# An expert block whose first stage is done by gathered rows, with its weights summed in DRAM

## The chip, the core and the metric

The kernel runs on one core of a Trainium2 chip. TensorE (PE) multiplies matrices, VectorE (DVE) and ScalarE (ACT) work on tiles of 128 partitions, GpSimd (POOL) works more slowly and issues the indirect transfers, and SyncE (SP) issues most of the plain ones. Each engine runs its instructions in a fixed order. The metric is the device time of the whole kernel in microseconds; lower is better.

## What is computed

One block of a language model works on 1,024 tokens of width 1,024 (eight blocks of 128 tokens). First come four mLSTM heads and four gMLP groups with an output projection; then a product-key layer (PEER) that picks, for each token and each of eight heads, 16 of 16,384 experts. The change touches only the second:

```python
s1, i1 = lax.top_k(s[:, :, 0], 16); s2, i2 = lax.top_k(s[:, :, 1], 16)
top_s, pos = lax.top_k(s1[..., :, None] + s2[..., None, :], 16)   # 16 of 16*16
idx  = i1 * 128 + i2 (at pos)                  # expert of the token: 8 heads x 16
gate = softmax(top_s)
a    = gelu(einsum('td,thkd->thk', x, expert_u[idx]))
out  = einsum('thk,thkd->td', a * gate, expert_v[idx])
```

## The kernel before

**Two ways through the experts.** A block can take the *sparse* way: for each of its 128 (head, choice) pairs, GpSimd gathers 128 rows of `u` (one for each token, 4 KB each) and VectorE takes the dot product with the normalised token (`dot`, L691 to L697); the same again with rows of `v`, weighted and added up (`add`, L707 to L713). Or it can take the *dense* way: every expert is computed for every token by TensorE, and a table of gates, zero for the experts that were not picked, is multiplied in. Blocks 0 to 4 are dense and blocks 5 to 7 sparse (`DENSE`, `SPARSE`).

**The front** (`front_part`, L563) works through parts of 2, 3 and 3 blocks: heads and groups, output projection, then the queries and scores of the experts. Weights come in half by half through three buffers (`wraw`, `split_w`, L66), each matrix is split into a high and a low part, and a product takes three matmuls (`mm3`, L89). The choice of experts of a block (`topk_units`, L452) and, for a dense block, its gate table (`gate_units`, L642) are side work: lists of small steps that `interleave` deals out between the main steps of the next part, the whole list within the first 210 cost units of that part. A gate step (a *quad*, four tokens) makes two tables of ones with VectorE (`AB`, L656), scales one with ScalarE (L659) and multiplies them on TensorE (`pG`, L661); 32 quads make a block's table, written to `d_G` in DRAM. The last list of side work is the choice of experts of block 5, which the main path runs itself.

**The dense stage** (`experts`, L755) has 128 expert rows of 128 experts, in 32 groups of four. `stage1` loads a row of `uT` (L777), splits it into `uhi` (ScalarE, L778) and `ulo` (GpSimd, L779), multiplies it with the 640 dense tokens in two halves of 320 columns (`pa`), and makes weights `wh`, `wl` of it with the gates `Gin`, which are loaded once a group (L771). `stage2` loads and splits four rows of `v` and adds their product to the accumulators of five blocks (`pout`, 2 x 512 columns for each block). The sparse blocks are side work of this stage: their gathers, dots and adds are dealt out between the expert rows, through seven row buffers (`gat`).

**What sets the order.** The code is emitted in the order of these loops, and a scheduler places the instructions of every engine by its own timeline of the program; `keep_in_program_order` pins the gathers among each other, and `high_priority` lifts a few steps. What the chip then does is in order, engine by engine.

Of the kernel before, what the change touches and what calls it, by code (L numbers as in the profile page):

```python
# [7 lines left out]
F32 = mybir.dt.float32  # L8
F32R = mybir.dt.float32r
# [7 lines left out]
DRAM = bass.MemoryType.DRAM  # L17

D = 1024
# [6 lines left out]
TG = 32  # L26

DENSE = [0, 1, 2, 3, 4]
SPARSE = [5, 6, 7]
# [11 lines left out]
NGAT = 4  # L41
# [5 lines left out]
class Build:  # L47
# [124 lines left out]
    def consts(self, cp):  # L172
# [9 lines left out]
        self.rall = cp.tile([128, 8], F32, name="rall", tag="rall")  # L182
        self.mhalf = cp.tile([128, 16], F32, name="mhalf", tag="mhalf")
# [269 lines left out]
    def topk_units(self, blk):  # L453
# [15 lines left out]
        def merge(h0):  # L469
            ijg = st["ijg"]  # L470
            self.merge16(h0, st["tv"], st["ti"], ijg)
            if blk in self.sparse:
                if h0 == 0:
                    self.pick[blk] = (self.kp.tile([128, 128], I32, name="ix", tag=f"ix{blk % 2}"),
                                      self.kp.tile([128, 128], F32, name="gt", tag=f"gt{blk % 2}"))
                ix, gt = self.pick[blk]
                hl = slice(h0 * 16, (h0 + HB) * 16)
                v.scalar_tensor_tensor(ix[:, hl], ijg[:, 0, hl], float(NEXP), ijg[:, 1, hl], op0=OP.mult, op1=OP.add)
                v.tensor_copy(gt[:, hl], ijg[:, 2, hl])

        def done():
            ijg = st["ijg"]
            if blk in self.dense:
# [74 lines left out]
    def front_part(self, part):  # L558
# [61 lines left out]
        for b in range(self.nb):  # L620
            blk = b0 + b
            if blk in self.dense:
# [19 lines left out]
    def gate_units(self, blk):  # L642
        nc = self.nc
        pool = self.gp
        s = self.dense.index(blk)
# [29 lines left out]

    def sparse_units(self, blk, pool, psum):
# [4 lines left out]
        def begin():  # L681
            st["ix"], st["gt"] = self.pick[blk]
# [55 lines left out]
    def open_x(self):  # L738
# [4 lines left out]
        T = len(self.dense) * 128  # L743
        self.xh = self.xp.tile([128, 8, T], F32R, name="xh", tag="xh")
        self.xl = self.xp.tile([128, 8, T], F32R, name="xl", tag="xl")
        for s, blk in enumerate(self.dense):
# [9 lines left out]
    def experts(self, side, dp, ps):  # L756
# [5 lines left out]
        T = ND * 128  # L762
        T2 = T // 2
        n32 = T // TG
        ngroups = NEXP // GS
        W, V, st = {}, {}, {"n": 0}

        def stage1(g, e):
            if e == 0:
                st["G"] = dp.tile([128, n32, GS, TG], F32, name="Gin", tag="Gin", bufs=1)  # L770
                nc.sync.dma_start(st["G"], self.d_G[:, :, g * GS:(g + 1) * GS].rearrange("n j i t -> j n i t"))  # L771
            G = st["G"]
# [9 lines left out]
            for s in range(2):  # L782
                pa = ps.tile([128, T2], F32, name="pa", tag="pa", bufs=3)
                sl = slice(s * T2, (s + 1) * T2)
                self.mm3(pa, [((uh[:, c], ul[:, c]), (xh[:, c, sl], xl[:, c, sl])) for c in range(8)])
                with self.first():
                    nc.scalar.activation(pa, pa, AF.Gelu_apprx_tanh)  # L787
                    p3 = pa.rearrange("p (n t) -> p n t", t=TG)
                    v.tensor_tensor(p3, p3, G[:, s * (n32 // 2):(s + 1) * (n32 // 2), e], op=OP.mult)  # L789
                    nc.scalar.activation(wh[:, sl], pa, AF.Copy)  # L790
                    v.tensor_sub(wl[:, sl], pa, wh[:, sl].bitcast(F32))  # L791
# [207 lines left out]
```

## Time and profile before

| | us |
|---|---|
| median of three runs | 2869.16 (2865.69 to 2877.17) |
| profiled execution | 2870.66 |
| its span | 2868.9 |
| busy in it: TensorE | 2707.1 (94%) |
| VectorE | 2198.3 (77%) |
| GpSimd | 1498.8 (52%) |
| ScalarE | 1120.5 (39%) |

The span is that of the profiled execution on the chip; the time around it is 1.8 us. Busy shares are means over stages with different limits, so they are read stage by stage below. Matmuls overlap, so that the duration of one is longer than its share of the time: their price is the step from one start to the next. "Idle before" names what ended an engine's wait.

### The profile page before, as it was taken

The page shows a single profiled execution, that of the slowest core. Times are in us where ns is not written, and L with a number is a line of the kernel's source. Part 1 is how long each engine was busy: PE and PEld are TensorE (multiplying, and loading weights), DVE is VectorE, ACT ScalarE, POOL GpSimd, SP SyncE. Part 2 cuts the span into 40 slices and gives each one's busy share as a digit, 9 for nine tenths or more (in the row PEclk, how much of TensorE's full clock was granted, in tenths as well). Part 3 has the DMA queues.
Part 4 walks back from the last instruction along what each step waited for, and adds up shares of the span by engine and source line. Part 5 has one row for each costly group of instructions (what it writes and reads, how often), then busy time and mean ns, then how long its engine had stood idle before and what let it go on. Part 6 is the DMA issues. An engine that isn't in the chain of part 4 may idle for free.

```text
span 2868.9 us, 44783 instructions
## 1 busy us (share of the span) xinstructions
PE 2707.1 (94%) x16283; PEld 2468.9 (86%) x16283; DVE 2198.3 (77%) x4981; ACT 1120.5 (39%) x2295; POOL 1498.8 (52%) x1220
## 2 busy tenths in 40 slices
PE   7888989999898799999999999999999999999998
PEld 7887989889898798889888888888888898889987
DVE  6649975289985677888797787978987777777774
ACT  5444788348888322223222222222222222222222
POOL 4430020000200186767767677667767777777873
PEclk9989999999999899999999999999999999999999
DMA  7797557866578798988989999898989999999992
GB/s 252 253 315 281 187 216 278 277 223 226 186 274 312 257 328 299 335 313 311 326 282 331 338 322 330 300 344 302 316 284 342 343 330 332 331 322 326 336 320 111
DMA packets 327821, 838.41 MB, mean 292 GB/s; under 512 B 25520, under 2 KB 161072, under 8 KB 315824
## 3 DMA queue, kind: packets, MB, share of 16 engines
q0 software_dynamic: 114048, 427.87, 40.4%
q1 hardware_dynamic: 190544, 347.91, 37.0%
q10 hardware_dynamic: 23008, 59.77, 5.3%
q8 instruction: 128, 2.10, 0.3%
q14 instruction: 93, 0.76, 0.1%
HBM read 746.32 MB, written 89.13 MB: 291 GB/s over the span
## 4 chain that ended last, share of the span: by engine, by line
PE 58%; DVE 19%; DMA 9%; ACT 5%; issue 5%; POOL 3%; SPq 1%; ACTq 1%; another core or an unknown queue 0%; POOLq 0%; DVEq 0%
PE pa L96 8%; PE pa L94 7%; PE pa L95 7%; PE pout L94 7%; PE pout L95 7%; PE pout L96 7%; DMA Gin<-d_G 4%; DVE gat L697 2%; PE pG L661 2%; DVE sacc L713 2%; DVE AB L656 2%; PE pq L94 2%; PE pq L96 2%; PE pq L95 2%; DMA wraw<-win 1%
## 5 line engine op out<-in xcount | busy, mean ns | idle before, releaser
L94 PE MATMUL pa<-xh,uhi 128*128 128x320 f32 x2048 | 639.3, 312 | 28.9 <-ACT uhi L778 14.9
L95 PE MATMUL pa<-xl,uhi 128*128 128x320 f32 x2048 | 637.1, 311 | 0.0
L96 PE MATMUL pa<-xh,ulo 128*128 128x320 f32 x2048 | 625.5, 311 | 5.4 <-POOL ulo L779 5.4
L94 PE MATMUL pout<-vhi,wh 128*128 128x512 f32 x1280 | 505.4, 400 | 23.0 <-DVE acc L816 11.1
L713 DVE SCALAR_TENSOR_TENSOR sacc<-gat,aw,sacc 128x1024 f32<-128x1024 f32 x384 | 492.3, 1282 | 27.4 <-DMA gat<-v,ix 22.3
L95 PE MATMUL pout<-vlo,wh 128*128 128x512 f32 x1280 | 509.0, 399 | 0.0
L96 PE MATMUL pout<-vhi,wl 128*128 128x512 f32 x1280 | 490.2, 398 | 0.0
L709 POOL DMA_INDIRECT gat<-v,ix x384 | 363.5, 947 | 239.8 <-DVE sacc L713 131.0
L697 DVE SCALAR_TENSOR_TENSOR gat<-gat,xn 128x1024 f32<-128x1024 f32 x384 | 459.5, 1213 | 20.0 <-DMA gat<-u,ix 19.8
L693 POOL DMA_INDIRECT gat<-u,ix x384 | 363.3, 946 | 209.5 <-DVE gat L697 104.3
L94 PEld LDWEIGHTS pa<-xh,uhi 128*128 128x128 f32 x2048 | 389.2, 190 | 43.2 <-DVE wl L791 16.1
L96 PEld LDWEIGHTS pa<-xh,ulo 128*128 128x128 f32 x2048 | 385.7, 190 | 12.9 <-POOL ulo L779 8.2
L95 PEld LDWEIGHTS pa<-xl,uhi 128*128 128x128 f32 x2048 | 389.3, 190 | 7.3
L779 POOL TENSOR_TENSOR ulo<-raw,uhi 128x1024 fp32r<-128x1024 f32 x128 | 308.7, 2413 | 145.6 <-ACT uhi L778 142.9
L801 ACT ACTIVATE vhi<-raw 128x1024 fp32r<-128x1024 f32 x128 | 131.7, 1052 | 487.5 <-PE pout L95 414.8
L802 POOL TENSOR_TENSOR vlo<-raw,vhi 128x1024 fp32r<-128x1024 f32 x128 | 307.9, 2416 | 22.7 <-ACT vhi L801 20.3
L94 PEld LDWEIGHTS pout<-vhi,wh 128*128 128x128 f32 x1280 | 242.0, 190 | 78.8 <-DVE acc L816 14.4
L816 DVE TENSOR_TENSOR acc<-acc,pout 128x512 f32<-128x512 f32 x320 | 214.2, 682 | 113.8 <-PE pout L96 89.9
L96 PEld LDWEIGHTS pout<-vhi,wl 128*128 128x128 f32 x1280 | 241.0, 190 | 54.0 <-DVE wl L791 0.4
L95 PEld LDWEIGHTS pout<-vlo,wh 128*128 128x128 f32 x1280 | 242.9, 190 | 50.2
L789 DVE TENSOR_TENSOR pa<-pa,Gin 128x320 f32<-128x320 f32 x256 | 126.7, 495 | 191.5 <-ACT pa L787 104.9
L790 ACT ACTIVATE wh<-pa 128x320 fp32r<-128x320 f32 x256 | 111.6, 436 | 379.0 <-DVE pa L789 315.0
(243 smaller groups left out, 5037.8 us busy)
## 6 DMA issues: line engine op xcount, KB each, us to landing
raw<-uT SPq DMA_DIRECT2D x128, 512.0 KB
raw<-v SPq DMA_DIRECT2D x128, 512.0 KB
wlo<-d_wl SPq DMA_DIRECT2D x48, 1024.0 KB
d_G<-Gt ACTq DMA_DIRECT2D x20, 2048.0 KB
Gin<-d_G SPq DMA_DIRECT2D x32, 1280.0 KB
wraw<-win SPq DMA_DIRECT2D x72, 512.0 KB
d_wl<-wlo POOLq DMA_DIRECT2D x24, 1024.0 KB
wraw<-wq SPq DMA_DIRECT2D x48, 512.0 KB
```

Source lines behind the costliest of these rows:

```text
L94: te.matmul(ps, lh, rh, start=k == 0, stop=False)
L95: te.matmul(ps, lh, rl, start=False, stop=False)
L96: te.matmul(ps, ll, rh, start=False, stop=k == n - 1)
L693: gd = nc.gpsimd.indirect_dma_start(out=t, out_offset=None, in_=self.I["u"], in_offset=bass.IndirectOffsetOnAxis(ap=st["ix"][:, k:k + 1], ...
L697: v.scalar_tensor_tensor(t, t, 1.0, st["xn"], op0=OP.mult, op1=OP.mult, accum_out=st["a"][:, k:k + 1])
L709: gd = nc.gpsimd.indirect_dma_start(out=t, out_offset=None, in_=self.I["v"], in_offset=bass.IndirectOffsetOnAxis(ap=st["ix"][:, k:k + 1], ...
L713: v.scalar_tensor_tensor(st["acc"], t, st["a"][:, k:k + 1], st["acc"], op0=OP.mult, op1=OP.add)
L779: nc.gpsimd.tensor_tensor(ul, ur, uh.bitcast(F32), op=OP.subtract)
L789: v.tensor_tensor(p3, p3, G[:, s * (n32 // 2):(s + 1) * (n32 // 2), e], op=OP.mult)
L801: nc.scalar.activation(vh, vr, AF.Copy)
L802: nc.gpsimd.tensor_tensor(vl, vr, vh.bitcast(F32), op=OP.subtract)
L816: v.tensor_add(st["acc"][:, s, dl], st["acc"][:, s, dl], po)
```

## The change

Block 0 becomes *mixed*. Its first stage goes the sparse way, but in the front: 128 gathers of rows of `u` with 128 dots on VectorE (`dot_units`), through two row buffers (`drow`). After each head, ScalarE and VectorE make the weights gelu(a) * gate of its 16 choices, and 16 indirect transfers of GpSimd add them to a table `d_M[j, i, t]` in DRAM, 128 single elements each (one for each token). The adds of one head don't wait for each other, but for all those of the head before; the table is zeroed first by four transfers from SP's queue. Its second stage stays dense: `stage1` loads four rows of `d_M` a group (`Min`), after the last adds, splits them into `mh` and `ml`, and `stage2` takes its weights for block 0 from there. So the first dense stage holds four blocks: `pa` is one product of 512 columns in place of two of 320, `d_G` and `Gin` are smaller by a fifth, and block 0 needs no gate quads. The first 90 steps of the new list are merged into the side work of part 1, the others into that of part 2. A fifth `gat` buffer takes some of the room that comes free.

```diff
+MIXED = 0
+EARLY = 90
-NGAT = 4
+NGAT = 5
+        nc.vector.scalar_tensor_tensor(junk, self.ident, 1.0, iota, op0=OP.mult, op1=OP.mult, accum_out=self.pcol)
...
+                if blk == MIXED:
+                    at = tk.tile([128, 16 * HB], F32, name="at", tag="at", bufs=1)
+                    v.tensor_scalar(at, ijg[:, 0, hl], 128.0, self.pcol, op0=OP.mult, op1=OP.add)
+                    v.scalar_tensor_tensor(self.place[:, hl], ijg[:, 1, hl], 128.0 * NEXP, at, op0=OP.mult, op1=OP.add)
...
+    def dot_units(self, blk):
+        def dot(k):
+            t = row()
+            gd = nc.gpsimd.indirect_dma_start(out=t, out_offset=None, in_=self.I["u"],
+                                              in_offset=bass.IndirectOffsetOnAxis(ap=ix[:, k:k + 1], axis=0))
+            self.tc.keep_in_program_order(gd)
+            v.scalar_tensor_tensor(t, t, 1.0, st["xn"], op0=OP.mult, op1=OP.mult, accum_out=st["a"][:, k:k + 1])
+        def clear(q):
+            out = flat[:, q * 4096:(q + 1) * 4096].rearrange("j (a c) -> j a c", c=1024)
+            d = nc.sync.dma_start(out, st["z"][:, None, :].to_broadcast([128, 4, 1024]))
+        def weigh(h):
+            nc.scalar.activation(a, a, AF.Gelu_apprx_tanh)
+            v.tensor_mul(a, a, self.slots[blk][1][:, hl])
+        def add(h, q):
+            for k in range(h * 16 + q * 4, h * 16 + q * 4 + 4):
+                gd = nc.gpsimd.indirect_dma_start(out=cells, in_=st["a"][:, k:k + 1], in_offset=None, compute_op=OP.add,
+                                                  out_offset=bass.IndirectOffsetOnAxis(ap=self.place[:, k:k + 1], axis=0))
+                tc.keep_in_program_order(gd)
+                tc.declare_no_dep(d, group=key, reason="the experts of one head of a token differ, tokens differ")
+                for e in self.added:
+                    tc.add_manual_dep(d, e.name, SYNC, reason="after the head before")
+        L = [begin] + [lambda q=q: clear(q) for q in range(4)]
+        for h in range(8):
+            L += [lambda k=k: dot(k) for k in range(h * 16, h * 16 + 16)] + [lambda h=h: weigh(h)]
+            if h:
+                L += [lambda h=h, q=q: add(h - 1, q) for q in range(4)]
+        return L + [lambda q=q: add(7, q) for q in range(4)]
...
         def stage1(g, e):
+                raw = dp.tile([128, GS, 128], F32, name="Min", tag="Min", bufs=1)
+                d = nc.sync.dma_start(raw, self.d_M[:, g * GS:(g + 1) * GS])
+                nc.scalar.activation(mh, raw, AF.Copy)
+                nc.gpsimd.tensor_tensor(ml, raw, mh.bitcast(F32), op=OP.subtract)
...
-            for s in range(2):
-                pa = ps.tile([128, T2], F32, name="pa", tag="pa", bufs=3)
-                self.mm3(pa, [((uh[:, c], ul[:, c]), (xh[:, c, sl], xl[:, c, sl])) for c in range(8)])
+            pa = ps.tile([128, T], F32, name="pa", tag="pa", bufs=3)
+            self.mm3(pa, [((uh[:, c], ul[:, c]), (xh[:, c], xl[:, c])) for c in range(8)])
...
-                prev = self.gate_units(blk)
+                prev = [] if blk == MIXED else self.gate_units(blk)
+        if b0 <= MIXED < b0 + nb:
+            dots = self.dot_units(MIXED)
+            self.left = dots[EARLY:]
+            return merged(dots[:EARLY], side)
+        side, self.left = merged(side, self.left), []
```

Where the new steps come to stand is the scheduler's choice. On SP's queue at the start of the program, before (`win` are the weights of the heads; `x3` is three in a row):

```order
L581 DMA nat<-x 128x1024 x2
L76 DMA wraw<-win 128x1024 x3
L312 DMA mg<-mng 128x128 x2
L388 DMA lng<-lng 128x128
L391 DMA ws<-ws 128x128 x2
L423 DMA kk<-keys 128x256 x2
L76 DMA wraw<-win 128x1024 x8
L388 DMA lnb<-lnb 128x128
```

and after:

```order
L595 DMA nat<-x 128x1024 x2
L79 DMA wraw<-win 128x1024 x3
L319 DMA mg<-mng 128x128 x2
L395 DMA lng<-lng 128x128
L398 DMA ws<-ws 128x128 x2
L430 DMA kk<-keys 128x256 x2
L722 DMA d_M<-zero 128x4x1024 x4
L704 DMA drow<-n2row 128x1024
L79 DMA wraw<-win 128x1024 x6
```

The four transfers that zero `d_M`, emitted with part 1's side work, have moved up to the fourth weight load of part 0.

On GpSimd where the front ends and the dense stage begins, before (`rall` is the norm of the last part's blocks):

```order
L62 TENSOR_SCALAR rall<-ss 128x1
L63 TENSOR_TENSOR rall<-rall,mhalf 128x1
L779 TENSOR_TENSOR ulo<-raw,uhi 128x1024 x2
L693 DMA gat<-u,ix 128x1024 x5
L779 TENSOR_TENSOR ulo<-raw,uhi 128x1024
L693 DMA gat<-u,ix 128x1024 x2
```

and after:

```order
L66 TENSOR_TENSOR rall<-rall,mhalf 128x1 x2
L710 DMA drow<-u,ix 128x1024 x12
L737 DMA d_M<-daw,place 2097152x1
L710 DMA drow<-u,ix 128x1024 x2
L737 DMA d_M<-daw,place 2097152x1 x15
L710 DMA drow<-u,ix 128x1024 x14
L737 DMA d_M<-daw,place 2097152x1 x17
L858 TENSOR_TENSOR ml<-Min,mh 128x512
L866 TENSOR_TENSOR ulo<-raw,uhi 128x1024 x2
L774 DMA gat<-u,ix 128x1024 x5
```

The last 28 gathers of block 0, the last 33 adds and the first `ml` now stand between the norm and the first `ulo`.

On VectorE in part 2, near the output projection (`nat`), before:

```order
L656 TENSOR_TENSOR AB<-iota,ijgT 128x1024
L537 TENSOR_TENSOR oh<-oh 128x256
L610 TENSOR_TENSOR nat<-xr,po 128x256
L537 TENSOR_TENSOR oh<-oh 128x128
L538 TENSOR_TENSOR ijg<-oh 128x16x4
L656 TENSOR_TENSOR AB<-iota,ijgT 128x1024
```

and after:

```order
L624 TENSOR_TENSOR nat<-xr,po 128x256
L729 TENSOR_TENSOR daw<-daw,gt 128x16
L568 MAX cs<-s_9360 128x8
L713 SCALAR_TENSOR_TENSOR drow,daw<-drow,dxn 128x1024
L670 TENSOR_TENSOR AB<-iota,ijgT 128x1024
```

The dots of block 0 (`drow,daw`) have come between the gate steps and the choice of experts, which stay where they were.

## Rows read from the trace of the kernel before

**Rows 1.** Busy us by stretch, with instructions, granted clock, transfer share, GB/s

```profile
core 0: us, PE busy (x) PEld busy (x) DVE busy (x) ACT busy (x) POOL busy (x), PEclk, DMA share, GB/s
20.00:40.00 20.00, 16.41 (x112) 16.03 (x112) 15.00 (x29) 9.95 (x13) 10.96 (x10) 0.84 0.89 282
180.00:520.00 340.00, 313.45 (x2305) 293.83 (x2304) 250.51 (x837) 233.73 (x561) 47.14 (x56) 0.97 0.70 250
520.00:980.00 460.00, 418.05 (x2942) 399.65 (x2942) 340.61 (x1307) 315.62 (x773) 27.36 (x40) 0.97 0.69 244
600.00:840.00 240.00, 222.61 (x1683) 211.25 (x1684) 229.75 (x874) 188.65 (x475) 23.66 (x30) 0.99 0.61 219
980.00:2830.00 1850.00, 1799.78 (x9852) 1615.68 (x9853) 1480.94 (x2573) 479.11 (x788) 1343.93 (x1028) 0.98 0.90 319
1600.00:1700.00 100.00, 98.81 (x533) 87.23 (x532) 77.47 (x135) 23.36 (x41) 72.20 (x58) 1.00 0.96 343
2320.00:2340.00 20.00, 19.50 (x98) 16.53 (x97) 14.68 (x26) 2.69 (x5) 13.81 (x12) 1.00 1.06 379
```

**Rows 2.** Timeline of TensorE in the dense stage: start us, us, engine, line, operation

```profile
2205.48 0.31 PE L94 MATMUL pa<-xh,uhi 128*128 128x320 f32 x1
...
2208.57 0.31 PE L94 MATMUL pa<-xh,uhi 128*128 128x320 f32 x1
...
2215.38 0.39 PE L96 MATMUL pout<-vhi,wl 128*128 128x512 f32 x1
...
2219.81 0.40 PE L94 MATMUL pout<-vhi,wh 128*128 128x512 f32 x1
```

**Rows 3.** Loads of the gate table: ns min/median/max, first and last start us

```profile
L771 SPq DMA_DIRECT2D Gin<-d_G x32: 377/377/404, 976.7 to 2780.8; - x32
```

**Rows 4.** Transfers from 1030 to 2780 us

```profile
DMA packets 222191, 562.66 MB, mean 322 GB/s; under 512 B 16564, under 2 KB 95156, under 8 KB 222069
```

**Rows 5.** Groups by line and shape: busy us, mean ns of one, idle before

```profile
L697 DVE SCALAR_TENSOR_TENSOR gat<-gat,xn 128x1024 f32<-128x1024 f32 x384 | 459.5, 1213 | 20.0 <-DMA gat<-u,ix 19.8
L779 POOL TENSOR_TENSOR ulo<-raw,uhi 128x1024 fp32r<-128x1024 f32 x128 | 308.7, 2413 | 145.6 <-ACT uhi L778 142.9 <-issue 0.7
L816 DVE TENSOR_TENSOR acc<-acc,pout 128x512 f32<-128x512 f32 x320 | 214.2, 682 | 113.8 <-PE pout L96 89.9 <-issue 22.8 <-PE pout L95 0.5
L656 DVE TENSOR_TENSOR AB<-iota,ijgT 128x1024 f32<-128x1024 f32 x160 | 196.0, 1231 | 58.8 <-PE pG L661 46.6 <-ACT sc L446 5.7 <-ACT AB L659 2.4
L789 DVE TENSOR_TENSOR pa<-pa,Gin 128x320 f32<-128x320 f32 x256 | 126.7, 495 | 191.5 <-ACT pa L787 104.9 <-DMA Gin<-d_G 55.1 <-issue 22.5
L697 DVE DVE_READ_ACCUMULATOR gat<-gat,xn 128x1 f32 x384 | 31.6, 82 | 0.0
```

**Rows 6.** Timeline of GpSimd: two gathers in a row

```profile
997.03 0.94 POOL L693 DMA_INDIRECT gat<-u,ix  x1 [0.30 <-issue]
998.27 0.93 POOL L693 DMA_INDIRECT gat<-u,ix  x1 [0.30 <-issue]
```

**Rows 7.** Timeline of SP's queue at the start, the fourth weight load first

```profile
19.48 23.75 SPq L76 DMA_DIRECT2D wraw<-win  x8
```

**Rows 8.** Chain that ended last, pieces of it: start us, us, what

```profile
25.07 6.25 DMA wraw<-win
...
596.54 3.88 DMA scb<-d_sc
...
1358.51 5.34 DMA gat<-v,ix
```

**Rows 9.** Timeline of TensorE in the front: a gate quad and its successor

```profile
938.39 1.05 PE L661 MATMUL pG<-AB 128*128 128x128 f32 x8
939.20 0.42 PE L95 MATMUL pq<-al,whi 128*128 128x384 f32 x1
```

**Rows 10.** Timeline of GpSimd at the front's end

```profile
987.82 4.93 POOL L779 TENSOR_TENSOR ulo<-raw,uhi 128x1024 fp32r<-128x1024 f32 x2 [140.86 <-ACT uhi L778]
```

**Rows 11.** Timeline of VectorE at the front's end

```profile
954.09 0.49 DVE L549 MAX8 tv<-scb 128x8 f32<-128x128 f32 x2 [9.02 <-DMA scb<-d_sc]
...
996.99 0.50 DVE L789 TENSOR_TENSOR pa<-pa,Gin 128x320 f32<-128x320 f32 x1
```

More of the change, by code (lines that the diff above doesn't have):

```diff
@@ L621, in front_part @@
             blk = b0 + b
-            if blk in self.dense:
+            if blk in self.dense[1:]:
                 bl = slice(b * 128, (b + 1) * 128)
@@ L644, in gate_units @@
         pool = self.gp
-        s = self.dense.index(blk)
+        s = self.dense.index(blk) - 1
         st = {}
@@ L742, in open_x @@
         self.xp = self.ctx.enter_context(self.tc.tile_pool(name="xparts", bufs=1, side="right", reuse_waits="tile"))
-        T = len(self.dense) * 128
+        T = (len(self.dense) - 1) * 128
         self.xh = self.xp.tile([128, 8, T], F32R, name="xh", tag="xh")
         self.xl = self.xp.tile([128, 8, T], F32R, name="xl", tag="xl")
-        for s, blk in enumerate(self.dense):
+        for s, blk in enumerate(self.dense[1:]):
             for src, dst in ((self.d_xh, self.xh), (self.d_xl, self.xl)):
@@ L761, in experts @@
         ND = len(self.dense)
-        T = ND * 128
-        T2 = T // 2
+        T = (ND - 1) * 128
         n32 = T // TG
         ngroups = NEXP // GS
-        W, V, st = {}, {}, {"n": 0}
+        W, V, M, st = {}, {}, {}, {"n": 0}
         def stage1(g, e):
@@ L771, in stage1 @@
                 nc.sync.dma_start(st["G"], self.d_G[:, :, g * GS:(g + 1) * GS].rearrange("n j i t -> j n i t"))
+                raw = dp.tile([128, GS, 128], F32, name="Min", tag="Min", bufs=1)
+                d = nc.sync.dma_start(raw, self.d_M[:, g * GS:(g + 1) * GS])
+                for f in self.added:
+                    self.tc.add_manual_dep(d.ins, f.name, SYNC, reason="after the last head")
+                mh, ml = st["M"] = tuple(dp.tile([128, GS, 128], F32R, name=n, tag=n, bufs=2) for n in ("mh", "ml"))
+                nc.scalar.activation(mh, raw, AF.Copy)
+                nc.gpsimd.tensor_tensor(ml, raw, mh.bitcast(F32), op=OP.subtract)
             G = st["G"]
@@ L811, in stage2 @@
                     dl = slice(d * 512, (d + 1) * 512)
-                    sl = slice(s * 128, (s + 1) * 128)
-                    self.mm3(po, [((W[i][0][:, sl], W[i][1][:, sl]), (V[i][0][:, dl], V[i][1][:, dl]))
-                                  for i in range(g * GS, (g + 1) * GS)])
+                    sl = slice((s - 1) * 128, s * 128)
+                    part = [[x[:, i % GS] if s == 0 else y[:, sl] for x, y in zip(M[g], W[i])]
+                            for i in range(g * GS, (g + 1) * GS)]
+                    self.mm3(po, [(w, (V[i][0][:, dl], V[i][1][:, dl]))
+                                  for w, i in zip(part, range(g * GS, (g + 1) * GS))])
                     with self.first():
```

69 lines of the change are left out of this document (52 added, 17 removed).

## The prediction

> **What bounds the kernel now.** I read the busy time by stretch first. The program has a front up to about 980 us (three parts of 2, 3 and 3 token blocks) and a dense stage behind it [rows 1]. In the dense stage TensorE is busy for 1,800 of 1,850 us at a granted clock of 0.98, VectorE for 80%, GpSimd for 73%, and the transfer engines have a share of 0.90. TensorE sets that pace, but three others stand close behind. The timeline of TensorE gives the price of its work: from 2205.48 to 2208.57 stand 21 steps of 320 columns, 0.147 us each; from 2215.38 to 2219.81 stand 19 steps of 512 columns, 0.233 us each [rows 2]. A group of four expert rows has 192 of the first and 120 of the second: 28.2 + 28.0 = 56.2 us. The loads of the gate table are issued once a group, the first at 976.7 and the last at 2780.8: 1,804 / 31 = 58.2 us a group [rows 3]. So TensorE works 96.5% of the time there, and 32 groups make 1,862 us.
>
> The front is less plain. From 600 to 840 us VectorE is busy for 229.75 of 240 us beside a TensorE at 93%; from 180 to 520 it has 89 us to spare in all [rows 1].
>
> **Dense stage, what the change takes out.** The first stage now streams 512 columns (blocks 1 to 4) in one matmul in place of two with 320. A group then has 96 + 120 matmuls of 512 columns: 216 x 0.233 = 50.3 us, 5.9 us less. If TensorE alone counted, that would be 189 us. The other needs per group, after the change:
> - Transfers: 562.66 MB in 1,750 us [rows 4] are 18.7 MB a group, and the bytes stay (1,024 KB of G and 256 KB of M for 1,280 KB of G). The fastest stretch of 100 us, 1600 to 1700, moved 343 GB/s at a share of 0.96 [rows 1]; at that rate a group takes 54.5 us. A single stretch of 20 us reached 379 GB/s, which would give 49.4 us.
> - GpSimd: 24 gathers at a period of 1.24 us [rows 6] and eight subtractions at 2.41 us [rows 5] make 49.1 us, and the new `ml` (half the elements) adds 1.2 us: 50.3.
> - VectorE: 0.80 x 58.2 = 46.6 us; eight pairs of 128x320 at 0.495 each become four pairs of 128x512 at about 0.68, the price of `acc` [rows 5], 2.5 us less: 44.1.
>
> Three engines then need 50 us and the transfers 49 to 55. I take 54.9 us, next to the measured 343 GB/s, since nothing in the trace holds more for long: 3.3 x 32 = 106 us gained. Bounds: 53.0 us (166 gained), and 56.6 us (51 gained), where the queues coupled in fixed order give up most of it. The second-stage slices from `mh` and `ml` cost nothing: as many matmuls, as many columns. The copy into `mh` is hidden by ScalarE, busy for 26% here [rows 1]; without that cover it would be under 1 us a group. The fifth gather buffer can only help.
>
> The Trainium skill, "DMA: Bandwidth & Descriptors", section Specifications, puts the HBM limit of one core at about 358 GB/s. By it a group could not go below 52.3 us, an estimate, and the gain not above 190 us; the stretch at 379 GB/s lies over that figure for 20 us, so the trace doesn't show it as a hard wall.
>
> **Front, the clear.** 8.4 MB of zeros are written from SP's queue. By the order they stand behind the third half-weight load, ahead of the fourth, at the very start. In the kernel before, the fourth is asked for at 19.48 us [rows 7], and half-weight loads end waits of 6.25 us there [rows 8], while TensorE is already busy for 16.41 of 20 us [rows 1]. At 379 GB/s the zeros take 22 us, and every weight behind them on the queue waits. Part 0 has no cover for it, as three buffers can't run ahead. I take 17 us, bounds 10 and 24. The pass for `pcol` and the memset of the zeros are two VectorE steps in the first 20 us, about 1 us each without cover, hidden by the loads.
>
> **Front, part 1 (180 to 520 us).** Block 0's 32 gate quads go. A quad holds TensorE for 0.81 us (938.39 to 939.20, [rows 9]): 26 us; VectorE loses 32 x 1.231 = 39 us and gets, counted in the order from this part's gate scan to its last `al`, 37 dots of 1.213 + 0.082 = 1.295 us [rows 5], 48 us. TensorE is busy for 92% here, so the stretch gets shorter: 18 us gained, bounds 30 and 0. ScalarE, 69% busy, gets freer too. The 67 MB of gathered rows over some 800 us of the two parts are 84 GB/s beside 244 to 250 [rows 1]; the 330 in sum lie under the 343 reached later, and the 8.4 MB that block 0 no longer writes to G go off. I count nothing for them.
>
> **Front, part 2.** Between its gate scan and its last `al` VectorE keeps its AB work (72 for 73) and gets 50 dots: 65 us. The stretch had 10 us free from 600 to 840 and some 7 on either side, so 48 us are lost; bounds 25 (if dots drift to the lighter end) and 65.
>
> **Front, GpSimd's queue.** It was almost empty here (27 us busy in part 2, [rows 1]). Now it holds 128 gathers, each behind the VectorE dot that frees one of two rows, and eight blocks of 16 adds, 16 x 1.24 = 20 us each if an add costs what a gather does. Small steps of the main path (`rall`, `hrr`, `grr`, `vv`) stand in between and wait, and with them the transposes and heads that read them. The scheduler put most dots where they fit: 6 us, bounds 0 and 30.
>
> **Front, the end.** Here the order is plain. Before, the first `ulo` runs at 987.82 [rows 10] behind nothing on GpSimd. Now 14 gathers, 17 adds and `ml` stand ahead of it, and `ml` needs Min, which needs all adds. VectorE's last run without a wait on scores goes from 954.09 to 996.99 [rows 11] and now holds some 16 dots more, 21 us; the last dot stands about 4 us ahead of its end: 1,014. The weighing takes about 2 us (a guess at two short steps), 17 adds 21 us: 1,037. Then the last add must land and Min must load, each about 3.9 us by the load that ended a wait at 596.54 [rows 8], and be split, about 1.8 us (`ml` as half a subtraction, and the copy ahead of it): 1,046 for the first `ulo`, 58 us late. TensorE has nothing else then. Bounds: 30 (dots done early) and 75 (a landing of 5.34 us as a gather had at 1358.51, [rows 8], and dots spaced by it). An add itself is in no row; its price runs from 0.94 us to that 5.34.
>
> The Trainium skill, same page, Rules for kernel authors, says of many small transfers that under 64 KB one pays mostly overhead, and its fit gives about 2.0 us for a DMA of 512 bytes. An add moves 512 bytes, so the rule speaks against the change. No run here shows an add yet; at 2.0 us each, with eight in flight, the sum below would not change, and with none overlapped the end alone would be 13 us later.
>
> **Sum.** The profiled execution took 2870.66 us for a span of 2868.9; the median of the three is 2869.16, so the sum can be made on either. Front: 17 - 18 + 48 + 6 + 58 = 111 us lost. Dense stage: 106 gained. 2870 + 111 - 106 = **2875 us**. The two terms almost cancel, and each is uncertain by about 40 us.
>
> **Rivals.**
> - *The dense stage keeps TensorE's pace.* With the same 96.5% a group takes 52.1 us, 195 gained: 2870 + 111 - 195 = 2786. For: GpSimd and VectorE have room, and 379 GB/s was reached. Against: 52.1 us need 359 GB/s throughout.
> - *The adds are dear (slower).* Place: GpSimd's queue. If an add holds the queue 2.5 us in place of 1.24, each block takes 40 us: the end is 21 us later, and gathers and `rall` behind the blocks in the two parts some 55 us in sum: 2875 + 76 = 2951. It decides once an add costs over about 1.5 us (17 x 0.3 at the end and half as much again at the blocks pass the half per cent). For: read and write of four bytes at 128 places. Against: a gather, as many descriptors, costs 0.94 us.
> - *The dense stage stays bound by its transfers (slower).* If the share can't go above 0.93, a group takes 18.7 MB / 330 GB/s = 56.7 us, 48 gained: 2933.
> - *The dots fit in beside TensorE,* VectorE's order having more slack than the busy share says: only the clear and the end are paid, 17 - 18 + 10 + 45 = 54: 2870 + 54 - 106 = 2818.
>
> That the change doesn't do what it says is excluded by the order: pa is 512 wide, block 0 has no quads left.
>
> **How the numbers follow.** About 0.5% is what a measurement of this kernel can tell from no change: 2855 to 2884. The forecast has 0.40 (its own range 2830 to 2920; 0.11 faster, 0.17 same, 0.12 slower). TensorE's pace 0.17, dots that fit in 0.11, both faster; dear adds 0.20, transfers 0.12, slower but for 0.02. Faster 0.39, same 0.19, slower 0.42. The range takes in half of the outermost two: 2785 to 2955.
>
> **What would show it.** Gate-table loads 54.9 us apart; the first pair of weight loads behind the zeros some 17 us late; AB and dots together at over 95% of VectorE in part 2; the first `ulo` at about 1,100 us on the new clock, behind adds 1.24 us apart. The prediction is wrong if the front is lengthened by under 70 us, if groups come 53 us apart or less, or if adds stand 2 us apart.

## The result: 5% slower, outside the range, and the profile after

The changed kernel takes 3014.93 us (median of four runs, 3006.96 to 3018.79) beside 2867.55 us before (four runs): 1.051 times as long, 95% interval 1.0474 to 1.0546. Forecast were 2875 us, with a range of 2785 to 2955. The profiled execution of after has a span of 3016.1 us, 147.2 more than before.

The quickest way to see where is a table of five milestones that both kernels pass: the first `win` load of part 1 and of part 2 on SP's queue, the end of the last scores on ScalarE, the start of the first `uhi`, and the start of TensorE's last `pout`. Each column is the time from one milestone to the next, the first from the start of the span, the last to its end.

| us | part 0 | part 1 | part 2 | end (scores to `uhi`) | TensorE's dense stage | behind it |
|---|---|---|---|---|---|---|
| before | 235.8 | 357.1 | 380.7 | 13.1 | 1871.8 | 10.4 |
| after | 243.5 | 391.4 | 500.0 | 95.8 | 1691.1 | 94.3 |
| difference | +7.7 | +34.3 | +119.3 | +82.7 | -180.7 | +83.9 |

The front is 244 us longer where 111 were forecast. The dense stage is 96.8 us shorter where 106 were forecast, but in two pieces that the forecast did not have: TensorE is done 181 us sooner, and then 84 us more of sparse work run alone.

Busy us by stretch, in the columns of [rows 1] (us, busy of PE, PEld, DVE, ACT, POOL, granted clock, DMA share, GB/s):

```profile
180.00:520.00 340.00, 281.54 (x2004) 261.59 (x2004) 249.98 (x882) 179.06 (x399) 133.91 (x115) 0.90 0.78 275
520.00:980.00 460.00, 352.90 (x2295) 329.62 (x2295) 340.56 (x1198) 239.49 (x567) 205.31 (x161) 0.87 0.74 250
600.00:840.00 240.00, 194.18 (x1287) 179.78 (x1286) 193.22 (x715) 129.73 (x301) 109.72 (x83) 0.91 0.76 251
1160.00:1200.00 40.00, 0.00 (x0) 0.00 (x0) 29.09 (x112) 1.75 (x3) 15.47 (x14) 0.50 0.56 168
...
2900.00:3000.00 100.00, 21.63 (x90) 16.52 (x90) 96.30 (x82) 5.75 (x10) 69.68 (x76) 0.63 0.96 376
```

From 600 to 840 VectorE was busy for 229.75 us before and is now for 193.22, beside a TensorE at 81% in place of 93% (part 2 begins at 592.9 before and at 634.9 now; in the 240 us from 635 VectorE is busy for 199.39). So it isn't VectorE's work that fills this stretch; VectorE waits too. The waits of TensorE from 200 to 1140 say where (us in total, times, longest):

```profile
PE pG L675 <- ACT AB L673: 57.9, 19, 13.3
PE tp L111 <- DVE diag L154: 38.5, 2, 23.3
PE pG L500 <- DVE ijg L552: 24.7, 2, 19.9
```

The longest of them, 23.3 us, can be followed from engine to engine. First GpSimd's timeline (start us, us, operation; in brackets the idle time before it), in which nearly every add is followed by the next after 0.30 us:

```profile
493.95 1.63 POOL L737 DMA_INDIRECT d_M<-daw,place  x1 [0.30 <-issue]
495.88 1.56 POOL L737 DMA_INDIRECT d_M<-daw,place  x1 [0.30 <-issue]
...
521.41 1.55 POOL L737 DMA_INDIRECT d_M<-daw,place  x1 [0.30 <-issue]
523.27 1.01 POOL L710 DMA_INDIRECT drow<-u,ix  x1 [0.30 <-issue]
524.36 0.19 POOL L65 TENSOR_SCALAR rall<-ss 128x1 f32<-128x1 f32 x1
```

then VectorE, which waits for that `rall`, and TensorE, which waits for VectorE's `diag`:

```profile
524.58 0.16 DVE L146 TENSOR_TENSOR ss<-s 128x1 f32<-128x1 f32 x1 [20.25 <-POOL rall L65]
...
527.19 2.99 PE L111 MATMUL tp<-diag,nat 128*128 128x128 f32 x12 [23.32 <-DVE diag L154]
```

These are 15 adds, most of them 1.86 us apart, and they hold GpSimd for 29 us. When the norm behind them comes, VectorE has waited 20.25 us for it, and TensorE's transposes 23.32 us for VectorE's `diag`. The other way in which a block hurts is that the gathers of the next rows stand behind it as well. GpSimd's timeline, then VectorE's:

```profile
1119.53 1.61 POOL L737 DMA_INDIRECT d_M<-daw,place  x1 [0.30 <-DVE tv L563]
...
1146.02 1.55 POOL L737 DMA_INDIRECT d_M<-daw,place  x1 [0.30 <-issue]
1147.88 1.00 POOL L710 DMA_INDIRECT drow<-u,ix  x1 [0.30 <-issue]
```

```profile
1135.22 0.68 DVE L549 TENSOR_TENSOR oh<-oh,ib 128x1024 bf16<-128x1024 bf16 x1
1152.07 1.23 DVE L713 SCALAR_TENSOR_TENSOR drow<-drow,dxn 128x1024 f32<-128x1024 f32 x1 [16.16 <-DMA drow<-u,ix]
```

VectorE stands for 16.16 us in front of a dot whose row has not come, with steps of the top-k queued behind it. Over the whole front the dots wait 94.3 us for their rows; in the run without adds, further down, it is 43.5, so about half of these waits come with the adds. The groups of the page (busy us, mean ns of one, idle before):

```profile
L710 POOL DMA_INDIRECT drow<-u,ix x128 | 151.1, 1180 | 438.7 <-DVE drow L713 210.9
L737 POOL DMA_INDIRECT d_M<-daw,place x128 | 216.3, 1690 | 45.1 <-issue 36.1
L713 DVE SCALAR_TENSOR_TENSOR drow<-drow,dxn 128x1024 f32<-128x1024 f32 x128 | 157.9, 1234 | 94.6 <-DMA drow<-u,ix 94.3
```

The end: the last scores leave ScalarE at 1134.9, and the first `uhi` starts at 1230.67. The timelines of GpSimd and ScalarE there:

```profile
1195.02 1.58 POOL L737 DMA_INDIRECT d_M<-daw,place  x1 [3.28 <-DVE oh L551]
...
1223.02 1.56 POOL L737 DMA_INDIRECT d_M<-daw,place  x1 [0.30 <-issue]
1229.51 1.25 POOL L858 TENSOR_TENSOR ml<-Min,mh 128x512 fp32r<-128x512 f32 x1 [4.94 <-ACT mh L857]
1231.81 4.70 POOL L866 TENSOR_TENSOR ulo<-raw,uhi 128x1024 fp32r<-128x1024 f32 x2 [1.04 <-ACT uhi L865]
```

```profile
1134.50 0.37 ACT L453 ACTIVATE sc<-psc 128x256 f32<-128x256 f32 x1
...
1228.80 0.63 ACT L857 ACTIVATE mh<-Min 128x512 fp32r<-128x512 f32 x1 [34.27 <-DMA Min<-d_M]
1230.67 2.00 ACT L865 ACTIVATE uhi<-raw 128x1024 fp32r<-128x1024 f32 x2 [1.24 <-DMA raw<-uT]
```

The dots run until 1194, the last 16 adds until 1224.6, then come the load of `d_M` (asked for at 1226.04) and, behind it on SP's queue, that of the first raw row (at 1226.42). TensorE does nothing from 1160 to 1200 (row above).

The dense stage, which answers [rows 3]: the gate loads, their second one, TensorE's last group of matmuls and VectorE a little later:

```profile
L851 SPq DMA_DIRECT2D Gin<-d_G x32: 377/377/560, 1164.0 to 2847.6; - x32
...
1265.97 0.43 SPq L851 DMA_DIRECT2D Gin<-d_G  x1
```

```profile
L99 PE MATMUL pout<-vhi,wl x1024: 388/394/796, 1254.2 to 2921.8; 128*128 128x512 f32 x171
...
2925.27 5.25 DVE L794 SCALAR_TENSOR_TENSOR sacc<-gat,aw,sacc 128x1024 f32<-128x1024 f32 x4
```

From the second load on, a group takes (2847.6 - 1266.0) / 30 = 52.7 us. Behind TensorE's last matmul VectorE adds up rows of the last sparse block, 96.30 us of the 100 from 2900 (row above). In GpSimd's order 68 of the 768 sparse gathers stand behind the last `vlo`; in the kernel before none does.

### The profile page after: what moved, and what is told of

Same layout as the page of the kernel before. It is cut to its first block, busy times and chain, and to the rows that moved or that the text cites. A ratio compares the mean times of both kernels' runs of the same rounds, so it can differ in the third digit from the quotient of the medians.

```text
span 3016.1 us, 38200 instructions
## 1 busy us (share of the span) xinstructions
PE 2535.4 (84%) x12952; PEld 2137.3 (71%) x12952; DVE 2259.4 (75%) x4969; ACT 1031.2 (34%) x1922; POOL 1912.1 (63%) x1508
## 5 line engine op out<-in xcount | busy, mean ns | idle before, releaser
L97 PE MATMUL pa<-xh,uhi 128*128 128x512 f32 x1024 | 407.7, 398 | 109.9 <-ACT uhi L865 109.8
L710 POOL DMA_INDIRECT drow<-u,ix x128 | 151.1, 1180 | 438.7 <-DVE drow L713 210.9
L97 PE MATMUL pout<-vhi,wh 128*128 128x512 f32 x1024 | 408.0, 398 | 16.6 <-DVE acc L903 9.8
L98 PE MATMUL pout<-vlo,wh 128*128 128x512 f32 x1024 | 406.5, 397 | 0.0
L98 PE MATMUL pa<-xl,uhi 128*128 128x512 f32 x1024 | 406.0, 396 | 0.0
L99 PE MATMUL pa<-xh,ulo 128*128 128x512 f32 x1024 | 400.5, 396 | 1.5 <-POOL ulo L866 1.4
L887 POOL TENSOR_TENSOR vlo<-raw,vhi 128x1024 fp32r<-128x1024 f32 x128 | 307.1, 2409 | 22.5 <-ACT vhi L886 21.0
L97 PEld LDWEIGHTS pa<-xh,uhi 128*128 128x128 f32 x1024 | 193.1, 189 | 162.1 <-ACT uhi L865 116.2
L737 POOL DMA_INDIRECT d_M<-daw,place x128 | 216.3, 1690 | 45.1 <-issue 36.1
L99 PEld LDWEIGHTS pout<-vhi,wl 128*128 128x128 f32 x1024 | 193.3, 189 | 52.7 <-DVE wl L876 5.9
L713 DVE SCALAR_TENSOR_TENSOR drow<-drow,dxn 128x1024 f32<-128x1024 f32 x128 | 157.9, 1234 | 94.6 <-DMA drow<-u,ix 94.3
L99 PEld LDWEIGHTS pa<-xh,ulo 128*128 128x128 f32 x1024 | 192.6, 188 | 50.1 <-POOL ulo L866 3.4
```

What stands on the lines that cost most here:

```text
L97: te.matmul(ps, lh, rh, start=k == 0, stop=False)
L98: te.matmul(ps, lh, rl, start=False, stop=False)
L99: te.matmul(ps, ll, rh, start=False, stop=k == n - 1)
L713: v.scalar_tensor_tensor(t, t, 1.0, st["xn"], op0=OP.mult, op1=OP.mult, accum_out=st["a"][:, k:k + 1])
L737: gd = nc.gpsimd.indirect_dma_start(out=cells, in_=st["a"][:, k:k + 1], in_offset=None, compute_op=OP.add, out_offset=bass.IndirectOffsetO ...
L887: nc.gpsimd.tensor_tensor(vl, vr, vh.bitcast(F32), op=OP.subtract)
```

## The experiments

Theory A, **the queue**: adds in a row hold GpSimd, and what stands behind them is late. Theory B, **the dots**: VectorE's dots and the round trip of their rows lengthen the front, and the adds lie beside them. For the dense stage: T, the transfers bound it; O, TensorE keeps its own pace and the tail is one of order.

All milestones, in the columns of the table above:

| run | us | part 0 | part 1 | part 2 | end | TensorE dense | behind |
|---|---|---|---|---|---|---|---|
| no adds | 2886.08 | 241.5 | 351.8 | 431.9 | 34.7 | 1719.2 | 96.0 |
| no dots | 2825.70 | 239.3 | 355.1 | 409.9 | 11.9 | 1708.9 | 98.1 |
| neither | 2752.78 | 242.5 | 320.0 | 369.5 | 11.4 | 1705.7 | 99.7 |
| adds spread | 2945.53 | 239.6 | 373.0 | 447.8 | 65.8 | 1714.3 | 98.5 |
| three raw buffers | 3112.07 | 243.2 | 387.2 | 505.5 | 59.8 | 1903.6 | 14.5 |
| plain writes | 2943.43 | 241.1 | 371.4 | 466.9 | 78.8 | 1689.9 | 93.6 |
| spread, deferred load | 2940.69 | 245.0 | 380.1 | 453.7 | 32.1 | 1800.7 | 35.2 |
| the same, dots late | 2966.84 | 242.5 | 371.9 | 455.8 | 62.6 | 1792.5 | 48.3 |
| the same, one gate load | 2934.23 | 244.9 | 371.1 | 450.9 | 32.2 | 1813.9 | 22.5 |
| no adds, half rows | 2816.97 | 242.1 | 349.5 | 415.2 | 12.0 | 1697.0 | 99.9 |
| no adds, four half rows | 2825.91 | 243.8 | 363.1 | 400.4 | 12.0 | 1702.1 | 102.6 |
| writes, spread | 2921.64 | 238.6 | 368.4 | 450.5 | 56.0 | 1706.7 | 97.8 |

The times are medians of one to eight runs, the milestones those of the profiled run alone, so that their sum can be some us off the median (11 in the run without adds).

**Adds left out.**

```diff
         def add(h, q):
+            return
```

> The 128 adds into d_M are left out (block 0's second stage then reads zeros); clear, gathers, dots, weighing and the dense stage stay. Theory A, the queue: 16 adds in a row hold GpSimd for 30 us, the gathers and small norm steps behind them come late, VectorE waits in order for the rows and TensorE for both. Then the waits of TensorE that were read in the front of the changed kernel (some 113 us) and about 50 us of the end go: 3015 - 163 = about 2850 us, 2830 to 2890. Theory B, the dots: 128 dots on VectorE with their round trip through two row buffers lengthen the front, the adds lie beside them. Then only the last 17 adds and their landing go, about 40 us: 2975 us, and not under 2950. Both: the gathers of the sparse blocks that stand behind the last vlo stay, so that some 90 us pass behind TensorE's last matmul.

2886.08 us, 1.0056 of before (1.0036 to 1.0076), at the upper end of what theory A allowed; theory B had nothing under 2950. The adds cost 129 us. Part 1 is 40 us shorter than after's, part 2 is 68, the end 61. Of these 169 us some 30 come back in the dense stage, which takes 1815 us here and 1805 to 1813 in the next three runs, but 1785 in after; why it is the shorter there stays open. TensorE's longest waits fall to these (200 to 1030):

```profile
PE pG L675 <- ACT AB L673: 15.2, 12, 2.5
PE pq L97 <- ACT qk L438: 11.2, 1, 11.2
```

**Dots left out**, and **both left out.**

```diff
         def begin():
+            v.memset(st["a"], 0.5)
...
         def dot(k):
+            return
```

> The 128 gathers and 128 dots of block 0 are left out (the sums are a constant 0.5); clear, weighing, adds and the dense stage stay. Theory A, the queue: no row can be late any more, but the norm steps still stand behind blocks of adds, some 60 us of waits of TensorE stay; the end costs little, as the last adds move up. Front 8 + 60 + 15 us longer than before, dense stage 97 us shorter: about 2855 us, 2820 to 2890. Theory B, the dots: the front is lengthened by the clear alone and gains 18 us by the gate quads: about 2765 us, not over 2800.

```diff
+        return [lambda q=q: clear(q) for q in range(4)]
         L = [begin] + [lambda q=q: clear(q) for q in range(4)]
```

> Gathers, dots, weighing and adds of block 0 are left out (its second stage reads zeros); the clear of d_M and the dense stage of four blocks stay. What the dense change is worth by itself: front some 10 us shorter (8 for the clear, 18 gained by 32 gate quads fewer), dense stage 97 us shorter with some 90 us behind TensorE's last matmul, since GpSimd's order keeps its gathers behind the last vlo: about 2765 us (both theories). If the sparse blocks' tail came from the longer front, it would be gone here and the time about 2700 us.

2825.70 us (0.9829 of before, 0.9793 to 0.9865) and 2752.78 us (0.9575, 0.9537 to 0.9614). With the run without adds these make a square. From the bare dense change, the dots alone (with their gathers and the weighing) cost 133 us, the adds alone 73, both together 262: 56 us belong to neither alone. The rows that are late behind the adds (94.3 us of waits in place of 43.5) are a cause that the traces show; that they are all of it isn't shown. Theory B alone falls (it had at most 2800 without dots), and so does the idea that the dots are cheap. The tail of 100 us is there with the shortest front as well, so it doesn't come from the front.

Part of the cost lies beside both theories, at TensorE's granted clock. The run with neither and after have the same matmuls in parts 1 and 2. First the two parts of after, then those of the run with neither (columns as above):

```profile
243.50:634.90 391.40, 314.45 (x2054) 293.19 (x2053) 261.37 (x941) 187.03 (x413) 146.08 (x130) 0.88 0.76 265
634.90:1134.90 500.00, 381.25 (x2561) 358.18 (x2559) 381.38 (x1250) 291.94 (x720) 223.40 (x167) 0.88 0.75 251
242.50:562.50 320.00, 295.37 (x2060) 278.75 (x2059) 210.30 (x861) 182.72 (x407) 29.32 (x44) 0.97 0.68 240
562.50:932.00 369.50, 352.67 (x2558) 336.17 (x2556) 303.14 (x1092) 280.07 (x710) 29.75 (x34) 0.98 0.68 248
```

In after TensorE stands still for 196 us of the two parts in place of 41, and it is busy for 696 us in place of 648, at a granted clock of 0.88 in place of 0.97 and 0.98. So 48 of the 202 us by which the two parts are longer are not waits: the same matmuls take longer. In the run without adds it is busy for 684 us at 0.94 and 0.93, 36 of 94. No run holds the clock apart from the waits, so its share alone isn't shown.

**Adds spread**, one behind each gather of the next head:

```diff
-EARLY = 90
+EARLY = 134
...
-            for k in range(h * 16 + q * 4, h * 16 + q * 4 + 4):
+            for k in (h * 16 + j,):
...
-            L += [lambda k=k: dot(k) for k in range(h * 16, h * 16 + 16)] + [lambda h=h: weigh(h)]
-            if h:
-                L += [lambda h=h, q=q: add(h - 1, q) for q in range(4)]
+            for j in range(16):
+                L += [lambda k=h * 16 + j: dot(k)]
+                if h:
+                    L += [lambda h=h, j=j: add(h - 1, j)]
+            L += [lambda h=h: weigh(h)]
```

> Everything is computed. The adds of a head are emitted one by one between the gathers of the next head, in place of four groups of four behind them; the first 134 steps (the same dots) stay in part 1. Theory A, the queue: a row is late by one add (1.9 us) in place of 16 (30 us), the norm steps too; what stays is the clear 8, dots on VectorE about 48 and the end about 70 us: 2870 + 126 - 97 = about 2900 us, 2870 to 2930. Theory B, the dots: as many dots through the same two buffers, 3000 us or more.

2945.53 us (1.0246 of before, 1.0192 to 1.03): 69 of the adds' 129 us come back with as many adds and dots (52 us in part 2, 18 in part 1 and 30 at the end, less 27 in the dense stage). That is far below the 3000 us of theory B, and 16 us over the range that theory A allowed (2870 to 2930): 60 us stay beside the run without adds, about half of them at the end, where 16 adds still stand in a row.

**Plain writes** in place of adds, in blocks and, with the same edit, in the version with spread adds:

```diff
-                gd = nc.gpsimd.indirect_dma_start(out=cells, in_=st["a"][:, k:k + 1], in_offset=None, compute_op=OP.add,
+                gd = nc.gpsimd.indirect_dma_start(out=cells, in_=st["a"][:, k:k + 1], in_offset=None,
```

> The 128 adds become plain indirect writes of the same 128 single elements (a later head then overwrites an earlier one at the same cell, so part of block 0's sums is left out). If it is the accumulation that costs GpSimd 1.56 us in place of a gather's 0.95, a write takes some 0.95, the queue is held 79 us less, and by the share that the adds cost so far (169 us of front for 238 of queue) the time is about 2960 us. If it is the elements (128 single addresses on the DRAM side), a write takes 1.56 too and the time stays at 3015 within 15.

> Spread one by one as in the version at 2945, and as plain writes (0.96 us) in place of adds (1.56 us): part of the sums is left out where a later head overwrites. The floor is the version without adds, 2886. If the adds cost by how long they hold GpSimd at a stretch, both cures help each other: a step behind it is late by 1.3 us at most, and 2895 to 2905 us are left. If they cost by the queue's total time, 128 x 0.6 = 77 us of 238 go, a third of the 60 that the spread adds cost: 2925 us.

One run of the first, 2943.43 us, and 2921.64 us for the second (1.0186, 1.0146 to 1.0227). The indirect transfers in the kernel with writes in blocks (duration ns min/median/max):

```profile
L737 POOL DMA_INDIRECT d_M<-daw,place x128: 954/972/4182, 371.8 to 1151.1; - x128
```

So a scatter of 128 single elements costs GpSimd 0.97 us, as a gather of 128 rows does, and the accumulation adds 0.59 (a median of 1561 ns in after). In blocks the shorter writes give back about 72 us (the first case, by 17 us more than expected), spread ones 24. By its time the last run is nearer to its second case, the queue's total time, but its milestones don't bear that out. Of the 21 us between the two profiled runs 10 come at the end, where 16 transfers still stand in a row (16 x 0.59 = 9 us), 8 in the dense stage and only 2 in parts 1 and 2. Why the spread transfers still cost 35 us in these two parts, beside the run without adds, is not shown by any run.

**Half rows**, without adds, through two buffers and through four in the same memory (`bufs=4`):

```diff
-            return self.fp.tile([128, D], F32, name="drow", tag="drow", bufs=2)
+            return self.fp.tile([128, 512], F32, name="drow", tag="drow", bufs=2)
...
-            v.scalar_tensor_tensor(t, t, 1.0, st["xn"], op0=OP.mult, op1=OP.mult, accum_out=st["a"][:, k:k + 1])
+            v.scalar_tensor_tensor(t, t, 1.0, st["xn"][:, :512], op0=OP.mult, op1=OP.mult, accum_out=st["a"][:, k:k + 1])
```

> The version without adds (2886), with rows of 512 elements gathered in place of 1024 and dots over 512 (half of each product is left out, and rows are others); still two row buffers. VectorE has some 77 us less to do in the front. Theory V, VectorE's busy time is what the dots cost (133 us beside the version without dots and adds): about half of it goes, 2825 us. Theory R, the round trip through two buffers (gather, landing of 5.5 us, dot) is what they cost: only the shorter dot and some landing go, 20 us: 2866 us.

> As the run with half rows, with four row buffers in the same memory; the same bytes, dots and gathers (half of each product is left out). Theory V: as that run, within 10 us. Theory R: VectorE doesn't wait for rows any more, and 40 us or more go beside that run, about 2800 us.

2816.97 us (0.9821, 0.9785 to 0.9858) and 2825.91 us (0.9853, 0.9816 to 0.9889). Half the work of a dot takes 69 us off, and twice the buffers takes nothing off, though the waits of the dots for their rows fall from 44.8 to 28.0 us (VectorE's idle time; first the run with two):

```profile
  DVE drow L713: 44.8, 28
```

```profile
  DVE drow L713: 28.0, 13
```

So the round trip through two buffers is not what the dots cost. By the total, half of VectorE's work is worth half of the 133 us, as theory V says. By stretch it is less plain. Of the 59 us between the profiled runs without adds, with full and with half rows, 23 come at the end, where no dot is left behind the scores, 18 in the dense stage, and only 19 in parts 1 and 2, where the dots cost 94. The other 75 us there don't go with the length of a dot or the number of buffers, and what they go with stays open; 26 of them are TensorE's same matmuls again, busy for 674 us in place of 648. (Half rows also move half the bytes, which these two runs don't separate from the dots.)

**The end and the tail**, in the version with spread adds: the load of `d_M` and its split behind stage1's four rows, and block 0 last in stage2:

```diff
         def stage1(g, e):
-                raw = dp.tile([128, GS, 128], F32, name="Min", tag="Min", bufs=1)
...
         def stage2(g):
...
                 V[i] = (vh, vl)
+            raw = dp.tile([128, GS, 128], F32, name="Min", tag="Min", bufs=1)
...
-            for s in range(ND):
+            for s in list(range(1, ND)) + [0]:
```

> The version with spread adds (2945), with the load of d_M and its split moved behind the four rows of stage1 and the v loads, and block 0 last in stage2. Everything is computed. The end: of the 66 us between the last scores and the first uhi, the raw loads no longer stand behind the adds on SP's queue; the gate table was asked for at 1076, so the first uhi at about 1080 in place of 1126, 46 us gained. Rival: the dense tiles lie in the memory of the front's rows and wait for the last adds anyway, 5 us gained. The tail: here 24 gathers stand behind the last vlo in place of 68. Theory O: 40 to 60 us of tail go with TensorE's pace kept, about 2850 us in all. Theory T: TensorE's groups get longer by as much, about 2900 us.

2940.69 us (1.0251, 1.0172 to 1.0331), the same as without it and over both cases of the expectation. The first `uhi` does come 34 us sooner behind the scores, but its `ulo` stands on GpSimd behind the last adds, and TensorE waits 28.1 us for it:

```profile
1138.28 1.54 POOL L737 DMA_INDIRECT d_M<-daw,place  x1 [0.30 <-issue]
1139.29 5.24 POOL L861 TENSOR_TENSOR ulo<-raw,uhi 128x1024 fp32r<-128x1024 f32 x2
```

And the tail: with 24 gathers behind the last `vlo` in place of 68 or more it is 63 us shorter, and TensorE's stage is 86 us longer, 28 of them that wait. Seen by its sum, that looks like theory T.

**T, directly**: the same with one gate load.

```diff
-            if e == 0:
+            if e == 0 and g == 0:
                 st["G"] = dp.tile([128, n32, GS, TG], F32, name="Gin", tag="Gin", bufs=1)
```

> The version with the deferred load, but the gate table is loaded for the first group only, and all groups use it (31 loads of 1.05 MB are left out, so the gates are wrong; no other work goes). Theory T, the transfers: 32.5 MB less at the 327 GB/s that every dense stage so far moved are 99 us: 2940 - 99 = about 2840 us, with TensorE's groups 3 us shorter. Theory E, the engines and their order set the pace of the dense stage: no change, 2920 us or more.

2934.23 us (1.023, 1.0185 to 1.0275): 32.5 MB less, and the dense stage takes 1836.4 us as it did with them. Theory T falls for this order of work, as far as it says that the stage lasts as long as its bytes. The order is not quite the same: the scheduler has also moved the last 24 gathers, so that none stands behind the last `vlo`. TensorE and VectorE then wait as follows (1130 or 1150 to 2750):

```profile
PE pout L97 <- ACT wh L870: 57.5, 20, 10.7
```

```profile
DVE sacc L796 <- DMA gat<-v,ix: 46.5, 31, 5.7
DVE gat L780 <- DMA gat<-u,ix: 25.4, 15, 5.2
```

VectorE stands 71.9 us in front of sparse rows that haven't landed (38.2 with all gate loads, 9.8 in after), and the multiplication of `pa` that makes `wh` is queued behind them. Gathers that are put off are free until TensorE is done; put ahead, they cost it about as much. Whether another order of the two could save the tail is open.

**Three raw buffers.**

```diff
-NRAW2 = 2
+NRAW2 = 1
```

> The changed kernel with three buffers for raw rows of uT and v in the dense stage in place of four (the scheduler then puts the sparse gathers earlier: none stands behind the last vlo on GpSimd, before it were 68). Theory T, the transfers: the dense stage is bound by the bytes that it moves, and the 94 us behind TensorE's last matmul are gathers that were put off, not time lost. Then TensorE's groups come 55 to 56 us apart in place of 52.7, the tail shrinks to some 15 us, and the whole stays at 3015 within 20 us. Theory O, the order: TensorE's pace of 52.7 us is not touched by the sparse blocks, and only the tail goes: 3015 - 80 = 2935 us. If TensorE is starved by the missing buffer, over 3040.

3112.07 us (1.0849, 1.0793 to 1.0904): the tail is gone and TensorE is starved (103.6 us of waits for `vlo`), the third case of the expectation. It tells nothing on T and O.

**Dots over the whole part**, from the version with the deferred load: the dots of heads 0 to 5 are spaced over all of part 1, the others over part 2.

```diff
...
-                    self.interleave(self.front_part(part), side, FTOT)
+                    self.interleave(self.front_part(part), side, FTOT, self.dots.pop(0) if self.dots else ())
```

> As the version with the deferred load, but the dots of heads 0 to 5 are dealt over the whole of part 1 and those of heads 6 and 7 over the rest of part 2, in place of the first 63% of each part, where VectorE is full. Everything is computed. If VectorE's busy time is what the dots cost (94 us of the two parts by the versions without adds), the light ends of the parts take up about half of it: 50 us less than the version with the deferred load. If the round trip through two row buffers sets their pace (a dot each 4 us or more), the front doesn't get shorter: within 15 us of that version.

2966.84 us (1.0343, 1.0259 to 1.0427), 26 above that version. The test is inconclusive: the scheduler placed 47 dots before part 2, fewer than the 53 of the version with the deferred load, so that the light end of part 1 was not filled.

## Why the prediction was wrong, step by step

**The GpSimd queue, the step that failed.** It was given 6 us (0 to 30). The adds cost 40 us in part 1 and 68 in part 2 (after less the run without adds), 108 us in place of 6. The prediction saw that small steps of the main path "stand in between and wait", and took 1.24 us for an add on the ground that a gather has as many descriptors. It is 1.86 us, and that alone is not the error: its own rival of dear adds, which decides from 1.5 us on, would have given at 1.86 about half of its 76 us. It priced GpSimd's time. It did not price that VectorE, in order, stands in front of a dot whose gather is behind a block of adds, or of a norm that is, with the top-k, gate and `diag` steps behind it. [rows 1] showed GpSimd almost idle in the front, which says that it has time, not that it can be held for 29 us without harm. Nor has the sum a term for TensorE's clock: it is made at the granted clock of before, 0.97 in the front [rows 1], and after has 0.88 there.

**The end, 58 us (30 to 75), was 83.** The places were right: the dots' end, the adds in a row, their landing, the load, the split. The 17 adds were 32 us and not 21, and the dots ended 59 us behind the scores (1194 to 1135) where the sum has 40 (1,014 to 973.6), as the rows were late. Without adds the end is 35 us, without dots and adds 11.

**Part 2, 48 us for the dots (25 to 65), came out at 51** without adds, and in part by luck. VectorE was full there, as forecast, for 145.75 of the first 151 us:

```profile
591.00:742.00 151.00, 134.00 (x871) 119.01 (x872) 145.75 (x514) 90.80 (x211) 39.41 (x39) 0.94 0.79 282
```

But the 51 are 62 for the dots, less 11 by which the run with neither is shorter than before, which the sum doesn't have, and half of a dot's work gave back only 17 of the 62. **Part 1, -18 (-30 to 0), was -5 without adds** (34 with them), in the range, by two errors that nearly cancel: the gate quads gave 37 and not 26 (the run with neither), and the dots took 32 where the sum leaves 8. **The clear, 17 us (10 to 24), was too dear:** the first `wq` load of part 0 came 14.6 us later (155.8 for 141.2), and 7.7 were left at the start of part 1.

**The dense stage, -106, was -97, and for another reason.** It was taken as bound by transfers at 343 GB/s, 54.9 us a group. The groups came 52.7 us apart, which is the rival of TensorE's pace (52.1) and one of the prediction's own signs that it is wrong (53 or less); [rows 4] moved 322 GB/s before, and after does 329 from 1250 to 2900:

```profile
DMA packets 207683, 543.56 MB, mean 329 GB/s; under 512 B 16448, under 2 KB 81728, under 8 KB 207583
```

What the prediction had no term for is that the sparse blocks fell behind: a group holds about 22 gathers in the new order of GpSimd, not 24. It compared each engine's need for a group with 24 gathers and didn't look at the order's last stretch. There the tail can be counted: some 70 gathers at VectorE's 1.3 us are 91 us. TensorE's stage came out 75 us better than the sum and the tail 84 worse, and that the two nearly cancel is luck.

Added up, parts 1 and 2 came out at +154 where +36 were in the sum (118 more, of which the adds are 102), the end 25 more, the clear 9 less, the dense stage 9 more: 143 us, the distance of the profiled execution (3017.92) from 2875.

**The cited rules.** "DMA: Bandwidth & Descriptors" of the Trainium skill (Rules for kernel authors) says that small transfers are mostly overhead, and it was the warning to be heard: an add moves 512 bytes and holds its queue for 1.56 us. The Trainium skill's fit of 2.0 us a transfer, on the same page, was read as a time in flight, which leaves the sum as it is; here the adds land after a median of 4.5 us, and it is the queue's time that hurts. The Trainium skill's limit of 358 GB/s (same page, Specifications) is exceeded for 20 us at a time, from 20 to 40 us where zeros are written beside the weight loads, and elsewhere without them (two rows of after, then one of before):

```profile
20.00:40.00 20.00, 15.15 (x82) 12.99 (x82) 11.97 (x36) 7.02 (x15) 5.09 (x6) 0.76 1.02 406
480.00:500.00 20.00, 20.00 (x173) 20.00 (x173) 10.34 (x18) 13.49 (x32) 8.89 (x7) 1.00 1.03 416
480.00:500.00 20.00, 17.63 (x135) 16.55 (x135) 9.01 (x16) 14.55 (x36) 3.26 (x6) 1.00 1.00 391
```

## What to carry to other kernels

An engine that is nearly idle can still be the one that hurts: what counts is how long it is held at a stretch, and which in-order engine stands behind it; spread between the gathers, the same adds cost half (60 us in place of 129). Before pricing a pipelined stage by what each engine needs, look at the end of the new order: work that stands there behind the last step of the bounding engine is a tail, and it can be counted. And the best that this change can give is what its cheap half gives alone: 118 us (77 in the dense stage, 37 in part 1 where the gate quads go), which the gathers, dots and weighing (133 us) already use up. No version that computes everything beat the kernel before.

## What the hardware showed that was not expected

- An indirect transfer that accumulates 128 single elements holds GpSimd for 1.56 us, the same transfer as a plain write for 0.97, a gather of 128 rows of 4 KB for 0.95.
- Over 20 us the transfers reached 416 GB/s in after (480 to 500) and 391 before, more than the 379 of [rows 1].
- 32.5 MB fewer loaded in the dense stage left its time at 1836 us, at a share of the transfer engines of 0.91 with them and 0.89 without (1130 to 2750; gathers had moved ahead there).
- The same matmuls of parts 1 and 2 kept TensorE busy for 648 us at a granted clock of 0.97 and 0.98, and for 696 at 0.88.
